# Hymba-style decoder step on one core: the up projection's seven-product scheme over all sixteen K tiles, operands and weight sums in place, residual summed in memory

## The chip, the cores and the metric

The kernel runs on one core of a Trainium2 chip. The time is device microseconds from one execution of the program, the median of three runs. The profile is of one further execution. Engines: TensorE (PE; its weight loads PEld), VectorE (DVE), ScalarE (ACT), GpSimd (POOL) and SyncE (SP), which here only issues transfers.

## What is computed

One layer over 512 prompt tokens and 8 x 4 sample tokens, 2048 channels, all in float32. Cut to what bears on this change:

```python
x = x + g1 * (concatenate([a_out, o]) @ w_out)             # output projection, residual
h2 = rms_norm(x, norm_ffn_g) * (1 + sc2) + sh2             # sc2, sh2, g2 come from c @ w_ada
u, f_tail = causal_dwconv(f_prev, h2 @ w_up, ffn_conv_w, ffn_conv_b)   # 2048 -> 2 x 5632, width 3
gate, val = split(u, 2)
x = x + g2 * ((silu(gate) * val) @ w_down)                 # 5632 -> 2048
```

Before it stand the input projection, a convolution group, windowed attention and the copies of two caches into the outputs; the change leaves these as they are.

## The kernel before

Channels lie on the 128 partitions, tokens along the free axis: 544 columns in two halves of 272 (256 prompt, 16 sample). Each float32 product is three matmuls: a weight tile and an activation tile are each split into a rounded part and a remainder (`split`, L344: ScalarE casts, VectorE subtracts), and hi x hi, hi x lo, lo x hi are added in PSUM. A weight split covers four tiles (128x512) and has three buffers of each part; raw weights come in 512 KB loads on SP's queue into three buffers (`load_w`, L192).

The sequence of the second half: `rest()` is the output projection, with the residual in two SBUF tiles `x2` and the sum of squares kept on VectorE; then `rstd2`; then the last `w_ada` stage, whose sixteen loads go through four buffers `raw_g`; then the sixteen channel tiles are normalised and modulated (`modulate2`). Tiles 8 to 15 are split as they are (`h2hi`, `h2lo`). Tiles 0 to 7 become seven operands of four tiles each (`sthi`, `stlo`): a two by two block scheme (gate and value outputs by two halves of K against two halves of K by two column halves) that needs seven block products in place of eight.

Each of the 44 pairs `f` (one gate and one value channel tile, `up_mm`) does the seven products over eight K tiles, 84 matmuls of 272 columns, with weight sums in separate buffers, and `direct` products over the other eight, 96 matmuls, into the same PSUM banks. The first pair takes its plain part from an array of its own (`w_up0`) before the seven products. Results are placed into `us` tiles; `up_conv` is the convolution (ScalarE the first tap, VectorE two more), then silu, product and split. After the first pair of each chunk of four comes the down product of the chunk before it (`down`): sixteen output tiles of 24 matmuls, each added with its gate into `x2` by VectorE (`gated_add`); the last one stores `x2` as the output `o_y` through ScalarE's queue.

The order on each engine is set when the program is built: a scheduler goes by program order and by which instruction is ready in its own estimate; on the chip each engine then takes its list in order. `shift_cache` puts one 1022 KB cache copy, memory to memory, behind a weight load on SP's queue.

## Time and profile before

| | before |
|---|---|
| median of three runs | 2668.88 us (2662.72 to 2673.99) |
| profiled execution, its own time | 2669.57 us |
| its span, first to last instruction | 2667.8 us |
| TensorE busy | 2603.1 us, 98%, 21073 matmuls |
| VectorE busy | 1655.6 us, 62% |
| ScalarE busy | 1082.9 us, 41% |
| GpSimd busy | 163.4 us, 6% |
| moved by DMA | 517.5 MB, mean 194 GB/s |

Matmuls are pipelined, so the mean time of one (about 290 ns) is longer than the distance between two; a stretch divided by its count of matmuls gives what one costs. The share of an engine is an average over stages with different limits.

### The profile page before, as it was taken

Reading aid. Unit: us, or ns where it says so; the run is one execution under the profiler, and the core shown is the slowest. Engines: PE = TensorE matmul, PEld = TensorE weight load, DVE = VectorE, ACT = ScalarE, POOL = GpSimd, SP = SyncE. Lnnn points to the kernel's source line nnn. Section 1 sums busy time; section 2 is a strip of 40 time slices with the busy share of each in tenths; the row PEclk is TensorE's granted clock in tenths of the full one; section 3 lists DMA queues with packets and bytes.
Section 4 is the critical chain, followed back from the end, with each engine's and each line's share of the span. In section 5 each row is a group of like instructions: output and inputs, shape, how many; then the busy total and the mean of one; then the engine's idle time right before and its main releaser. Section 6 shows DMA issues by size and latency. Waiting matters only on the chain.

```text
span 2667.8 us, 51885 instructions
## 1 busy us (share of the span) xinstructions
PE 2603.1 (98%) x21073; PEld 2380.3 (89%) x21073; DVE 1655.6 (62%) x3312; ACT 1082.9 (41%) x2069; POOL 163.4 (6%) x448
## 2 busy tenths in 40 slices
PE   6999999999999999789999999999999999999999
PEld 5878676778767799589999999999999999999999
DVE  5678754635665343676676766665757676666665
ACT  4355554445447332443343424242424242434332
POOL 0000000000000000010010101010101010100000
PEclk8999999999999999899999999999999999999999
DMA  9885567676764542445554555455455555554554
GB/s 352 278 277 160 187 199 261 227 257 226 244 224 158 179 153 88 142 163 192 182 191 167 192 182 191 167 192 182 173 185 192 182 173 186 190 183 169 192 186 140
DMA packets 119135, 517.50 MB, mean 194 GB/s; under 512 B 15728, under 2 KB 25584, under 8 KB 116080
## 3 DMA queue, kind: packets, MB, share of 16 engines
q1 hardware_dynamic: 103744, 494.98, 54.3%
q10 hardware_dynamic: 15152, 19.22, 2.1%
q8 instruction: 165, 2.70, 0.4%
q14 instruction: 74, 0.61, 0.1%
HBM read 503.18 MB, written 144.92 MB: 243 GB/s over the span
## 4 chain that ended last, share of the span: by engine, by line
PE 95%; DVE 2%; DMA 2%; ACT 1%; issue 0%; DVEq 0%; ACTq 0%
PE acc L207 47%; PE b L887 36%; PE x L272 4%; PE x L706 2%; PE x L657 2%; PE m L515 1%; PE m L445 1%; DMA raw_s<-w_ada 1%; PE m L480 1%; PE acc L324 1%; PE m L477 1%; PE m L498 1%; DMA raw_g<-w_ada 0%; DVE slo L346 0%; DVE qkr L320 0%
## 5 line engine op out<-in xcount | busy, mean ns | idle before, releaser
L345 ACT CAST whi<-raw_w 128x512 fp32r<-128x512 f32 x752 | 466.0, 620 | 888.9 <-PE acc L207 684.5
L346 DVE TENSOR_TENSOR wlo<-raw_w,whi 128x512 fp32r<-128x512 f32 x752 | 517.2, 688 | 347.5 <-ACT whi L345 336.6
L207 PE MATMUL acc<-hhi,whi 128*128 128x272 f32 x1792 | 393.1, 298 | 2.7 <-ACT hhi L345 2.3
L887 PE MATMUL b<-dhi,whi 128*128 128x272 f32 x1376 | 394.7, 289 | 0.0
L887 PE MATMUL b<-dlo,whi 128*128 128x272 f32 x1376 | 392.8, 288 | 0.0
L887 PE MATMUL b<-dhi,wlo 128*128 128x272 f32 x1376 | 384.3, 289 | 0.0
L207 PE MATMUL acc<-hhi,wlo 128*128 128x272 f32 x1792 | 382.6, 292 | 0.0
L207 PE MATMUL acc<-hlo,whi 128*128 128x272 f32 x1792 | 380.4, 292 | 0.0
L887 PE MATMUL b<-shi,whi 128*128 128x272 f32 x1232 | 358.5, 291 | 17.0 <-ACT whi L345 8.4
L887 PE MATMUL b<-slo,whi 128*128 128x272 f32 x1232 | 356.2, 289 | 1.5 <-DVE slo L346 1.5
L887 PE MATMUL b<-shi,wlo 128*128 128x272 f32 x1232 | 357.4, 290 | 0.0
L207 PEld LDWEIGHTS acc<-hhi,whi 128*128 128x128 f32 x1792 | 282.5, 189 | 53.2 <-issue 39.6
L207 PEld LDWEIGHTS acc<-hhi,wlo 128*128 128x128 f32 x1792 | 283.0, 190 | 22.4 <-issue 20.9
L207 PEld LDWEIGHTS acc<-hlo,whi 128*128 128x128 f32 x1792 | 283.2, 189 | 21.0 <-issue 18.5
L337 DVE SCALAR_TENSOR_TENSOR half<-acc,modT,half 128x512 f32<-128x512 f32 x200 | 150.1, 750 | 244.8 <-PE acc L207 244.7
L207 PE MATMUL acc<-alo,whi 128*128 128x272 f32 x1408 | 291.6, 288 | 0.0
L207 PE MATMUL acc<-ahi,whi 128*128 128x272 f32 x1408 | 290.6, 288 | 0.8 <-DVE tg L340 0.5
L207 PE MATMUL acc<-ahi,wlo 128*128 128x272 f32 x1408 | 290.9, 288 | 0.0
L887 PEld LDWEIGHTS b<-dlo,whi 128*128 128x128 f32 x1376 | 259.4, 189 | 0.0
L887 PEld LDWEIGHTS b<-dhi,whi 128*128 128x128 f32 x1376 | 259.3, 188 | 0.0
L887 PEld LDWEIGHTS b<-dhi,wlo 128*128 128x128 f32 x1376 | 253.5, 188 | 0.1
L887 PEld LDWEIGHTS b<-shi,whi 128*128 128x128 f32 x1232 | 232.8, 189 | 19.1 <-ACT whi L345 8.7
(207 smaller groups left out, 3694.5 us busy)
## 6 DMA issues: line engine op xcount, KB each, us to landing
raw_s<-w_ada SPq DMA_DIRECT2D x176, 512.0 KB, 4.8
raw_w<-w_up SPq DMA_DIRECT2D x176, 512.0 KB, 3.7
o_k_s<-cache_k SPq DMA_DIRECT2D x64, 1022.0 KB, 6.9
o_v_s<-cache_v SPq DMA_DIRECT2D x64, 1022.0 KB, 6.6
raw_w<-w_down SPq DMA_DIRECT2D x88, 512.0 KB, 3.7
raw_w<-w_in SPq DMA_DIRECT2D x80, 512.0 KB, 4.3
raw_s<-kT_c SPq DMA_DIRECT2D x64, 448.0 KB, 4.3
raw_s<-v_c SPq DMA_DIRECT2D x56, 512.0 KB, 4.5
```

What stands on the lines that cost most here:

```text
L207: nc.tensor.matmul(out[:, c, 0:HALF], lhsT=w, rhs=x[:, c, :], start=start and i == 0, stop=stop and i == 2)
L272: nc.tensor.matmul(ps[32 * j:32 * j + 9, 0:w], lhsT=silc[:, kt, :], rhs=t[:, c:c + w], start=kt == 0, stop=kt == KT - 1)
L324: nc.tensor.matmul(ps[:, c, 0:HALF], lhsT=w, rhs=src[:, c, :], start=start, stop=stop)
L337: nc.vector.scalar_tensor_tensor(pv(dst), pv(ps), modT[:, gate, 0:1], pv(dst), op0=ALU.mult, op1=ALU.add)
L345: nc.scalar.copy(hi, src)
L346: return nc.vector.tensor_tensor(lo, src, hi.bitcast(F32), op=ALU.subtract).ins
L445: nc.tensor.matmul(s_ps[:, 0:HALF], lhsT=blk, rhs=sq[:, c, :], start=True, stop=True)
L477: nc.tensor.matmul(s_ps, lhsT=lq, rhs=kr[rows[par], :, 0:HP], start=True, stop=True)
L480: nc.tensor.matmul(s_ps[:, 0:n0], lhsT=lq, rhs=kr[rows[par], 0, 0:n0], start=True, stop=True)
L657: nc.tensor.matmul(s_ps[32 * g:32 * g + 32, 0:hk], lhsT=qb[:, 2 * g + o, n, :], rhs=ks[g], start=o == 0 and n == 0, stop=o == 1 and n == 1 ...
L706: nc.tensor.matmul(o_ps[32 * g:32 * g + 32, :], lhsT=pT[0:w, c0:c0 + 32], rhs=rhs[g], start=kt == 0, stop=kt == 7)
L887: nc.tensor.matmul(out[:, 0:HALF], lhsT=w, rhs=x, start=start and i == 0, stop=stop and i == 2, skip_group_check=True)
```

## The change

- The seven-product scheme now covers all sixteen K tiles: seven operands of eight tiles (`B1`, `B2`, `T1` to `T3`; `T4` takes the place of the second half of `B1`). A pair is 7 x 8 x 3 = 168 matmuls. The first two pairs are plain products over all tiles and both halves (`direct`), 192 matmuls each.
- Normalisation, modulation and the block sums of the operands are done in place in `x2`, two or four tiles at a time, during the plain pairs: `plain` before each quarter of the first, `while_sums` before each quarter of the second. The convolution and product of these two pairs (`gated_act`) come after the pools they need are open, the first before the third pair, the second after it.
- Weight sums are done in place in the raw tiles, 1024 wide, with one extra tile `s1`; raw weights have two buffers more (`load_u`), and the loads' order is a11, a21, a22, a12.
- `x` is written to `o_y` during the output projection (`finished`); a down product's result is scaled by ScalarE into a tile `ym` (three buffers) and added into `o_y` in memory by an accumulating transfer issued by GpSimd.
- Twelve of the last `w_ada` stage's loads are issued during the output projection, the last square goes to the sum over partitions by itself, and pools are opened in another order.

```diff
-RAW_G = 4
-Q = 4
-XN = 3
+RAW_G = 12
+Q = 8
+YM = 3
...
+    mid.close()
+    o1 = ctx.enter_context(ExitStack())
     op = pool("op", bufs=4, to=o1, side="right")
+    o2 = ctx.enter_context(ExitStack())
+    og = pool("og", bufs=RAW_G, to=o2, side="right")
+    psf = pool("psf", bufs=4, space=PSUM)
     x2.append(half_tile())
...
+    def finished(m):
+        nc.scalar.dma_start(A["o_y"][m], x2[m // 8][:, m % 8])
...
+            finished(m)
+            if m < KT - 1:
+                sumsq(ssum2, x2[m // 8][:, m % 8], op, False)
+    last_ada = len(FIRST) + 7
+    raw_g = []
+    loads = ada_loads(last_ada, lambda: og.tile([P, 1024], F32, name="raw_g"))
+    for i, _ in enumerate(rest()):
+        if i >= 10 and len(raw_g) < RAW_G:
+            raw_g.append(next(loads))
+    ada = ada_stage(psf, op, last_ada, chain(raw_g, loads), main_ps())
+    for _ in range(6):
+        next(ada)
+    sq = wtile(op)
+    nc.scalar.activation(sq, x2[1][:, 7], AF.Square)
     ps = main_ps()
-    ones_sum(ps, ones, ssum2)
+    ones_sum(ps, ones, ssum2, True, False)
+    ones_sum(ps, ones, sq, False, True)
+    rstd2 = op.tile([P, 2, HALF], F32, name="ssum", bufs=1)
     rstd_from(ps, D, op, rstd2)
+    run(ada)
+    o2.close()
     hs.close()
+    fs = ctx.enter_context(ExitStack())
     hf = pool("hf", to=fs)
...
+    B1, B2 = operand("b1", 2), operand("b2", 2)
+    T1, T2, T3 = operand("t1"), operand("t2"), operand("t3")
+    B11, B21, B22, T4 = ([t[:, i] for t in b] for b, i in ((B1, 0), (B2, 0), (B2, 1), (B1, 1)))
+    def normalized(h, j, n):
+        x = x2[h][:, j:j + n]
+        v = x.rearrange("p k c n -> p k (c n)")
+        r = rstd2.rearrange("p (o c) n -> p o (c n)", o=1).broadcast_to([P, n, 2 * HALF])
+        nc.vector.tensor_tensor(v, v, r, op=ALU.mult)
+        k = 8 * h + j
+        for c in range(2):
+            xs = x[:, :, c, HP:HALF].rearrange("p k (b t) -> p k b t", t=DT)
+            for base, alu in ((SC2, ALU.mult), (SH2, ALU.add)):
+                m = modT[:, base + k:base + k + n, 1 + 4 * c:5 + 4 * c].rearrange("p k (b o) -> p k b o", o=1)
+                nc.vector.tensor_tensor(xs, xs, m.broadcast_to([P, n, DB // 2, DT]), op=alu)
+        for i in range(n):
+            nc.scalar.activation(pv(x[:, i]), pv(x[:, i]), AF.Identity, bias=modT[:, SH2 + k + i, 0:1],
+                                 scale=modT[:, SC2 + k + i, 0:1])
+    def blocks(h, j, n):
+        src = x2[h][:, j:j + n].rearrange("p k c n -> p c k n")
+        hi, lo = (b[:, :, j:j + n] for b in (B1, B2)[h])
+        split(hi, lo, src)
+    def combine(j, n):
+        b11, b12, b21, b22 = (x2[h][:, j:j + n, c] for h in range(2) for c in range(2))
+        nc.vector.tensor_tensor(b11, b12, b11, op=ALU.subtract)
+        yield
+        split(T1[0][:, j:j + n], T1[1][:, j:j + n], b11)
+        yield
+        nc.vector.tensor_tensor(b12, b22, b12, op=ALU.subtract)
+        yield
+        split(T3[0][:, j:j + n], T3[1][:, j:j + n], b12)
+        yield
+        nc.vector.tensor_tensor(b22, b22, b11, op=ALU.subtract)
+        yield
+        split(T2[0][:, j:j + n], T2[1][:, j:j + n], b22)
+        yield
+        nc.vector.tensor_tensor(b21, b21, b22, op=ALU.subtract)
+        yield
...
+    def direct(f, outs, before):
+        for h in range(2):
+            raws = [load_w(A["w_up"][t, h]) for t in (f, FT + f)]
+            shift_cache(raws[1][1])
+            for u in range(2):
+                before(h, u)
+                ws = [split_w(raw[:, u]) for raw, _ in raws]
+                for a in range(4):
+                    k = 4 * u + a
+                    for out, (hi, lo) in zip(outs, ws):
+                        for c in range(2):
+                            mm1(out[c], hi[:, a], lo[:, a], *(b[:, c, k] for b in (B1, B2)[h]),
+                                h == 0 and k == 0, h == 1 and k == 7)
+    for j in range(0, 4, 2):
+        normalized(0, j, 2)
+    def plain(h, u):
+        for j in (0, 2):
+            blocks(h, 4 * u + j, 2)
+            if (h, u) != (1, 1):
+                normalized(h + u, 4 * (1 - u) + j, 2)
+    first = [[bank(), bank()] for _ in range(2)]
+    direct(0, first, plain)
+    o1.close()
+    fe = pool("fe", to=fs)
...
+    def load_u(src):
+        nraw[0] += 1
+        if nraw[0] % 5 in (2, 4):
+            raw = fe.tile([P, 1024], F32, name="raw_x", bufs=2)
+            ins = nc.sync.dma_start(raw, src).ins
+            return raw.rearrange("p (u a m) -> p u a m", u=2, m=P), ins
+        return load_w(src)
...
+    st_in = state_tile(0)
+    us0 = placed(first, st_in, 0)
+    second = [main_ps(), main_ps()]
+    sums = chain(combine(0, 4), combine(4, 4))
+    def while_sums(h, u):
+        for _ in range(4):
+            next(sums, None)
+    direct(1, [[t[:, c] for c in range(2)] for t in second], while_sums)
+    run(sums)
+    for j in (0, 4):
+        split(T4[0][:, j:j + 4], T4[1][:, j:j + 4], x2[1][:, j:j + 4, 0])
+    hx.close()
+    fp = pool("fp", to=fs, side="right")
+    def product(out, w, b, start, stop):
+        for u in range(2):
+            hi, lo = split_w(w[:, u])
+            for a in range(4):
+                k = 4 * u + a
+                mm1(out, hi[:, a], lo[:, a], b[0][:, k], b[1][:, k], start and k == 0, stop and k == 7)
...
+    def up_mm(f, usg, usv):
+        a11, _ = load_u(A["w_up"][f, 0])
+        a21, _ = load_u(A["w_up"][FT + f, 0])
+        a22, ins = load_u(A["w_up"][FT + f, 1])
         shift_cache(ins)
-        a11, a12, a21, a22 = g0[:, 0], g0[:, 1], v0[:, 0], v0[:, 1]
-        s1, s2, s4 = (fp.tile([P, 4, P], F32, name="sum", bufs=3) for _ in range(3))
+        a12, ins = load_u(A["w_up"][f, 1])
+        shift_cache(ins)
+        s1 = fe.tile([P, 2, 4, P], F32, name="sum", bufs=1)
         b1 = bank()
-        product(b1, a11, 0, True, True)
+        product(b1, a11, B11, True, True)
         nc.vector.tensor_tensor(s1, a21, a22, op=ALU.add)
-        nc.vector.tensor_tensor(s2, s1, a11, op=ALU.subtract)
+        nc.vector.tensor_tensor(a21, a11, a21, op=ALU.subtract)
+        nc.vector.tensor_tensor(a11, s1, a11, op=ALU.subtract)
         b2 = bank()
-        product(b2, s2, 4, True, True)
-        p1 = part_tile("p1")
+        product(b2, a11, T2, True, True)
+        p1 = part_tile("p1", 2)
         nc.scalar.copy(p1, b1[:, 0:HALF])
         u2 = part_tile("u2")
         plus(u2, b2[:, 0:HALF], p1)
-        product(b1, a12, 1, False, early)
-        nc.vector.tensor_tensor(a21, a11, a21, op=ALU.subtract)
-        product(b2, a21, 5, False, True)
+        product(b1, a12, B21, False, True)
+        nc.vector.tensor_tensor(a12, a12, a11, op=ALU.subtract)
+        place(usg, 0, copied, b1)
+        product(b2, a21, T3, False, True)
         u3 = part_tile("u3")
         plus(u3, b2[:, 0:HALF], p1)
-        b4 = None
-        if not early:
-            b4 = bank()
-            g1, _ = load_w(A["w_up"][f, 1])
-            direct((b1, b4), g1, (False, True), (True, False))
-        place(usg, 0, copied, b1)
         b3 = bank()
-        product(b3, s1, 3, True, True)
+        product(b3, s1, T1, True, True)
         plus(u2, b3[:, 0:HALF], u2)
-        nc.vector.tensor_tensor(s4, a12, s2, op=ALU.subtract)
-        if early:
-            b4 = bank()
-        product(b4, s4, 2, early, True)
+        place(usv, 1, plus, b3, u3)
+        b4 = bank()
+        product(b4, a12, B22, True, True)
         place(usg, 1, plus, b4, u2)
         b5 = bank()
-        product(b5, a22, 6, True, early)
-        if not early:
-            v1, ins = load_w(A["w_up"][FT + f, 1])
-            shift_cache(ins)
-            direct((b5, b3), v1, (False, False), (True, True))
-        place(usv, 1, plus, b3, u3)
+        product(b5, a22, T4, True, True)
         place(usv, 0, plus, b5, u3)
...
+    def gated_act(f, usg, usv, tails, j):
         gt = up_conv(f, usg, tails, 2 * j)
         vl = up_conv(FT + f, usv, tails, 2 * j + 1)
         nc.scalar.activation(gt, gt, AF.Silu)
...
-    def down(c, last):
+    def up_pair(f, st_in, tails, j):
+        usg, usv = us_tile(st_in, 2 * j), us_tile(st_in, 2 * j + 1)
+        up_mm(f, usg, usv)
+        gated_act(f, usg, usv, tails, j)
+    def down(c):
         for mp in range(8):
-            raw, ins = load_w(A["w_down"][c, mp])
+            raw, ins = load_u(A["w_down"][c, mp])
             if mp % 2:
                 shift_cache(ins)
             for j in range(2):
...
                 for k in range(CHUNK):
                     ahi, alo = acts[CHUNK * c + k]
                     mm3(ps, hi[:, k, :], lo[:, k, :], ahi, alo, k == 0, k == CHUNK - 1)
-                xm = x2[m // 8][:, m % 8]
-                gated_add(xm, ps, G2 + m, fp)
-                if last:
-                    nc.scalar.dma_start(A["o_y"][m], xm)
+                ym = fp.tile([P, 2, HALF], F32, name="ym", bufs=YM)
+                nc.scalar.activation(pv(ym), pv(ps), AF.Copy, scale=modT[:, G2 + m, 0:1])
+                nc.vector.tensor_tensor(sv4(ym), sv4(ps), per_batch(modT[:, G2 + m, 1:9]), op=ALU.mult)
+                nc.gpsimd.dma_start(A["o_y"][m], ym, accum_op=ALU.add)
 
     for c in range(NCHUNK):
-        st_in = fp.tile([P, 2 * CHUNK, DB, 2], F32, name="st_in", bufs=2)
-        nc.scalar.dma_start(st_in, A["state_f"][c])
-        tails = fp.tile([P, 2 * CHUNK, 9, 2], F32, name="tails", bufs=2)
-        for j in range(CHUNK):
+        if c:
+            st_in = state_tile(c)
+        tails = fe.tile([P, 2 * CHUNK, 9, 2], F32, name="tails", bufs=2)
+        if c == 0:
+            gated_act(0, *us0, tails, 0)
+        for j in range(2 if c == 0 else 0, CHUNK):
             up_pair(CHUNK * c + j, st_in, tails, j)
+            if c == 0 and j == 2:
+                gated_act(1, *placed([[t[:, i] for i in range(2)] for t in second], st_in, 1), tails, 1)
             if c and j == 0:
-                down(c - 1, False)
+                down(c - 1)
         nc.scalar.dma_start(A["o_fc"][c], tails)
-    down(NCHUNK - 1, True)
+    down(NCHUNK - 1)
```

## Rows read from the trace of the kernel before

**Rows 1.** The page, part 1: busy us, share of the span, instructions.
```profile
PE 2603.1 (98%) x21073; PEld 2380.3 (89%) x21073; DVE 1655.6 (62%) x3312; ACT 1082.9 (41%) x2069; POOL 163.4 (6%) x448
```

**Rows 2.** The page, part 4: the chain that ended last, by engine and line.
```profile
PE 95%; DVE 2%; DMA 2%; ACT 1%; issue 0%; DVEq 0%; ACTq 0%
PE acc L207 47%; PE b L887 36%; PE x L272 4%; PE x L706 2%; PE x L657 2%; PE m L515 1%; PE m L445 1%; DMA raw_s<-w_ada 1%; PE m L480 1%; PE acc L324 1%; PE m L477 1%; PE m L498 1%; DMA raw_g<-w_ada 0%; DVE slo L346 0%; DVE qkr L320 0%
```

**Rows 3.** Stretches: length, busy PE, PEld, DVE, ACT, POOL (instructions), PE clock, DMA share, GB/s.
```profile
1088.50:1245.30 156.80, 132.42 (x1029) 120.69 (x1029) 118.81 (x246) 78.40 (x131) 15.56 (x40) 0.90 0.50 174
1245.30:2613.40 1368.10, 1367.41 (x10859) 1366.69 (x10858) 894.63 (x1849) 500.64 (x862) 109.89 (x310) 1.00 0.53 183
```

**Rows 4.** The page, part 5: costliest groups (count; busy us, mean ns; idle before).
```profile
L345 ACT CAST whi<-raw_w 128x512 fp32r<-128x512 f32 x752 | 466.0, 620 | 888.9 <-PE acc L207 684.5
L346 DVE TENSOR_TENSOR wlo<-raw_w,whi 128x512 fp32r<-128x512 f32 x752 | 517.2, 688 | 347.5 <-ACT whi L345 336.6
...
L887 PE MATMUL b<-dhi,whi 128*128 128x272 f32 x1376 | 394.7, 289 | 0.0
...
L887 PE MATMUL b<-shi,whi 128*128 128x272 f32 x1232 | 358.5, 291 | 17.0 <-ACT whi L345 8.4
```

**Rows 5.** Stretches: four consecutive up pairs.
```profile
1433.60:1524.10 90.50, 90.50 (x721) 90.50 (x720) 61.34 (x115) 39.64 (x71) 10.29 (x28) 1.00 0.54 190
```

**Rows 6.** Timeline of VectorE in an up pair (start us, us, instruction).
```profile
1474.37 0.69 DVE L929 TENSOR_TENSOR sum<-sum,raw_w 128x512 f32<-128x512 f32 x1
1474.97 0.69 DVE L346 TENSOR_TENSOR wlo<-raw_w,whi 128x512 fp32r<-128x512 f32 x1
```

**Rows 7.** Timeline after the output projection.
```profile
1090.85 0.72 DVE L320 TENSOR_TENSOR ssum<-ssum,w 128x544 f32<-128x544 f32 x1 [0.72 <-ACT w L319]
...
1095.86 0.72 DVE L306 SCALAR_TENSOR_TENSOR rstd<-w 128x544 f32<-128x544 f32 x1
1096.62 2.00 DVE L327 TENSOR_TENSOR xn<-half,rstd 128x544 f32<-128x544 f32 x3
...
1097.38 2.22 ACT L328 ACTIVATE xn<-xn,modT 128x512 f32<-128x512 f32 x3 [3.07 <-DVE xn L327]
...
1098.53 0.39 DVE L329 TENSOR_TENSOR xn<-xn,modT 128x32 f32<-128x32 f32 x3
```

**Rows 8.** VectorE's groups by form, 1433.6 to 1572.7 us.
```profile
L978 DVE SCALAR_TENSOR_TENSOR ca<-us,fw,ca 128x560 f32<-128x560 f32 x16 | 12.8, 799 | 1.8 <-ACT ca L976 1.7
...
L346 DVE TENSOR_TENSOR alo<-a,ahi 128x544 fp32r<-128x544 f32 x4 | 2.9, 717 | 0.0
...
L1000 DVE TENSOR_TENSOR a<-ca 128x512 f32<-128x512 f32 x4 | 2.7, 685 | 0.0
```

**Rows 9.** Stretches between the output projection and the up pairs.
```profile
1120.00:1130.00 10.00, 3.67 (x20) 2.61 (x18) 9.97 (x25) 7.34 (x12) 0.00 (x0) 0.80 0.00 0
...
1100.00:1140.00 40.00, 24.08 (x178) 16.96 (x174) 33.22 (x81) 23.94 (x37) 0.00 (x0) 0.76 0.30 100
```

**Rows 10.** The chain in order of time: start us, us, what.
```profile
1157.13 12.88 PE b L887 x99
```

**Rows 11.** Stretches: inside the output projection.
```profile
1040.00:1060.00 20.00, 20.00 (x162) 20.00 (x161) 8.01 (x15) 5.66 (x9) 0.00 (x0) 1.00 0.32 101
```

**Rows 12.** Issue of the stores of y: ns least, median, most.
```profile
L1027 ACTq DMA_DIRECT2D o_y<-half x16: 338/338/343, 2622.5 to 2664.8; - x16
```

**Rows 13.** Timeline of the end, VectorE.
```profile
2663.70 0.75 DVE L337 SCALAR_TENSOR_TENSOR half<-acc,modT,half 128x512 f32<-128x512 f32 x1 [1.94 <-PE acc L207]
```

**Rows 14.** DMA issues: count, KB each, median us to landing.
```profile
raw_w<-w_up SPq DMA_DIRECT2D x176, 512.0 KB, 3.7
o_k_s<-cache_k SPq DMA_DIRECT2D x64, 1022.0 KB, 6.9
...
o_y<-half ACTq DMA_DIRECT2D x16, 272.0 KB, 2.2
```

**Rows 15.** GpSimd's copies into the tails tile: ns least, median, most.
```profile
L973 POOL COPY tails<-us x88: 184/719/1391, 1155.3 to 2614.4; 128x2 f32<-128x2 f32 x88
```

More of the change, by code (lines that the diff above doesn't have):

```diff
@@ L175, in build @@
     g_ffn = params[:, 96 + KT:96 + 2 * KT]
[L176 removed]
+    cw = f32(qkp, [P, CT, W_CONV + 3], "cw")
     nc.scalar.dma_start(cw, A["conv_a"])
@@ L256, in interleave, with ada_loads, ada_stage @@
                 next(side, None)
-    def ada_stage(psp, tmp, s, get=None):
-        get = get or raw_tile
+    def ada_loads(s, get):
+        n = ADA_STAGES[s][2]
+        for i in range(KT * n // 4):
+            t = get()
+            nc.sync.dma_start(t, A[f"w_ada{s}"][i])
+            yield t
+    def ada_stage(psp, tmp, s, loaded=None, banks=None):
         t_a, t_b, n = ADA_STAGES[s]
@@ L263, in ada_stage @@
         per = 1024 // (groups * w)
-        ps = psp.tile([P, 512], F32, name="x", bufs=XB)
+        ps = banks[:, 0] if banks is not None else psp.tile([P, 512], F32, name="x", bufs=XB)
+        loaded = loaded or ada_loads(s, raw_tile)
         for i in range(KT // per):
-            t = get()
-            nc.sync.dma_start(t, A[f"w_ada{s}"][i])
+            t = next(loaded)
             for k in range(per):
@@ L279, in ada_stage @@
             copy(st[32 * j:32 * j + 9, 0:w], ps[32 * j:32 * j + 9, 0:w])
-        pt = psp.tile([P, 512], F32, name="m")
+        pt = banks[:, 1] if banks is not None else psp.tile([P, 512], F32, name="m")
         ns, nj = w // P, groups // 2
@@ L888, in mm1, with us_tile @@
                              skip_group_check=True)
[L890 to L902 removed]
+    def direct(f, outs, before):
[22 more added lines that the diff above has]
+    fe = pool("fe", to=fs)
+    fw = f32(fe, [P, UT, 4], "fw")
+    nc.scalar.dma_start(fw, A["ffn_conv"])
+    nraw = [0]
+    def load_u(src):
[5 more added lines that the diff above has]
+        return load_w(src)
+    def us_tile(st_in, slot):
+        us = fe.tile([P, UW], F32, name="us", bufs=2)
+        seg = us[:, USEG:].rearrange("p (b w) -> p b w", w=2 + DT)
+        nc.gpsimd.memset(us[:, 0:2], 0.0)
+        nc.gpsimd.tensor_copy(seg[:, :, 0:2], st_in[:, slot])
+        return us
     def place(us, c, op, ps, t=None):
@@ L915, in copied, with state_tile, placed @@
         nc.scalar.copy(out, ps)
-    def part_tile(name):
-        return fp.tile([P, HALF], F32, name=name, bufs=1)
-    def up_mm(f, usg, usv, early):
-        g0, _ = load_w(A["w_up"][f, 0])
-        v0, ins = load_w(A["w_up"][FT + f, 0])
+    def state_tile(c):
+        st_in = fe.tile([P, 2 * CHUNK, DB, 2], F32, name="st_in", bufs=2)
+        nc.scalar.dma_start(st_in, A["state_f"][c])
+        return st_in
+    def placed(outs, st_in, j):
+        uss = [us_tile(st_in, 2 * j + i) for i in range(2)]
+        for us, out in zip(uss, outs):
+            for c in range(2):
+                place(us, c, copied, out[c])
+        return uss
```

85 lines of the change are left out of this document (13 added, 72 removed).

## The prediction

> **What bounds the kernel now.** I read the shares of the engines first: TensorE is busy 98% of the span, VectorE 62% [rows 1]. Then the chain of waits: 95% of what ends last is TensorE, 47% its lines of projections and down products, 36% the line of the up products [rows 2]. Last the stretches: from the first down product (1245.3 us) to the end of the last up pair (2613.4 us) TensorE is busy 1367.4 of 1368.1 us at full clock, so there a matmul costs 1368.1 / 10859 = 0.126 us and nothing else counts. Before it, from the end of the output projection (1088.5) to 1245.3, it is busy 132 of 156.8 us at a mean clock of 0.90 [rows 3]. That is the one stretch where waits cost: 900 up matmuls at 0.126 are 113 us, so 43 us go to other things. The profiled execution took 2669.57 us, 0.7 over the median of the runs; I sum on it and take 0.7 off.
>
> **The change part by part.**
>
> *Fewer matmuls.* Of the old up projection the plain half is 3 x 1376 matmuls, the seven-product half 3 x 1232 [rows 4]; with 96 of the first pair that another line issues, 7920, or 180 a pair. New: two plain pairs of 192 (16 K tiles, two outputs, two column blocks, three terms), and 42 pairs of 7 x 8 x 3 = 168, in all 7440. The tile shape stays 128x272. In the TensorE-bound stretch stand 39 pairs: 39 x 12 x 0.126 = **59 us less**. The other 12 fall into the transition.
>
> *VectorE in a steady pair.* Four consecutive pairs take 90.5 us, VectorE 61.3 in them [rows 5], 15.3 a pair. A 512-wide operation starts 0.60 us after the one before it [rows 6], and three 544-wide ones take 2.00 us together, 0.64 apart [rows 7]; from the two, 1.1 ns an element, so one 1024 wide takes 1.16 us (at most 1.21, two narrow ones) and one 1088 wide 1.23. A pair now has 14 weight splits for 11 (+1.8) and four 1024-wide weight sums for four 512-wide (+2.2): 19.3 us in a pair of 168 x 0.126 = 21.2 us. VectorE is still hidden, but at 91%, not 68%. What is late next is the pair's second product: its weight difference (1.16) must wait until the first product's splits have read the tile it overwrites, and its own cast (0.62) and low part (0.69) follow [rows 4], while VectorE also has the convolution of the pair before, about 4.1 us (four taps 0.7 apart, product, split) [rows 8]. With three split buffers the second product's operand can be started about 1.5 us before the pair begins and is wanted at 3.0 us. Followed by hand it is between 0 and 0.75 us late, at the 29 of 39 pairs that don't follow a down product. Lower end 0 (nothing idles now). Upper end: VectorE no busier than 33.2 of 40 us, as it was where it set the pace [rows 9]; then a pair takes 19.3 / 0.83 = 23.3 us, 2.1 more, 61 us in all. I take 0.4 x 29 = **12 us**, near the lower end, since the work fits, and where enough stood ready VectorE was 9.97 of 10 us busy [rows 9].
>
> *Transition.* Now: last output product at 1088.5, square, sum and three Newton steps to 1096.6, then sixteen modulations, differences and splits on VectorE, until the up products run without a break from 1157 [rows 10]. New: the last square goes straight to TensorE (one 0.72 addition less), so the scale is there at 1095.9 [rows 7]; the w_ada products run under it, since twelve of sixteen loads are requested during the output projection, whose DMA share is 0.32 [rows 11]. These loads and sixteen stores of x pass SP's and ScalarE's queues there; they are hidden by that free share, and uncovered their issue alone would cost 28 x 0.34 = 9.5 us [rows 12]. First operands: two-tile product 1.23, sample columns 0.4, ScalarE 2 x 0.74, a cast of twice the width of one that takes 0.62 [rows 4], so 1.24 at most, and its low part 1.23: TensorE starts near 1101.5. VectorE then has, for plain pair one, 16 wide operations of 1.23, 32 small ones of 0.10 and 8 splits of 0.60: 27.7 us against 24.2 of TensorE; for plain pair two, 16 wide ones and 8 splits, 24.5 against 24.2; then two pairs of 19.3, with the two delayed convolutions, 8.2. Sum 99 us from 1095.9, then one more pair of 21.2 to the first down product: 1216 with VectorE never idle, 1236 at the 83% of [rows 9]. TensorE alone would allow 1101.5 + 888 x 0.126 = 1213. I take the middle of the VectorE figures, 1226, against 1245.3: **19 us less** (9 to 32).
>
> *Residual in memory.* A down product's evacuation leaves VectorE (0.75 us [rows 13]) for ScalarE (0.81, as its 512-wide scaling row [rows 7]) and a small VectorE multiply; ScalarE then has 0.62 + 0.81 of each 3.02 us, hidden under TensorE. GpSimd issues 176 accumulating transfers of 272 KB; behind each stand the zeroing and state copies of the next pair's tiles, wanted only 9 us into that pair. Three buffers allow 3 x 3.02 = 9.1 us from one use to the next, less 0.8 for ScalarE: 8.2 us for issue and landing. No row shows an accumulate. From below, the plain 272 KB store of y lands in 2.2 us; from above, a 1022 KB copy, memory to memory, in 6.9 [rows 14]. Both fit; I take 4 to 5, nearer the store by size, and nothing on the path. At the very end it shows: the last product ends at 2663.7 [rows 13], and 0.75 + 0.3 + store become 0.81 + issue + accumulate: **+2 us** (0 to +5).
>
> *Loads.* Five raw buffers for three; a pair holds four, the last until its seventh product's split, about 3.2 us before the pair ends. The next pair's fourth tile is requested then and wanted 6 us into it, against the 3.7 us to landing of such a load [rows 14]: nothing, or, if a cache copy is ahead of it, part of the 12 us above.
>
> Sum: 2669.6 - 59 - 19 + 12 + 2 = 2605.6, less 0.7: about **2605 us**.
>
> **The rivals.**
>
> *VectorE becomes the bound* (for it: 91% and longer chains; against: a long unbroken supply of splits). At 83% in both places: 2669.6 - 59 - 9 + 61 + 2 = 2665 us, no change.
>
> *The accumulates are too slow: slower.* If one takes longer than 8.2 us from issue to landing, ScalarE waits for the buffer, with the casts of the next weights behind it, and TensorE waits for both; each of 176 products takes a third of the excess longer. It decides from 8.2 + 3 x (64 / 176) = 9.3 us; at 12 us it costs 176 x 1.27 = 223 us: 2829 us. Against it: both transfers of [rows 14] lie below. For it: GpSimd's own rows, a two-element copy taking 0.18 to 1.39 us, median 0.72 [rows 15]. The Trainium skill (SBUF — State Buffer, section "Who interferes with whom") says that a VectorE instruction with two SBUF inputs holds the shared interface, and a GpSimd instruction that reads SBUF is blocked for its whole length, while one that only writes is not; the spread of that row agrees, and whether issuing an accumulate reads is shown by no run here. By the rule a blocked issue would use 1.2 of the 8.2 us and move the deciding landing to 8.1.
>
> *TensorE alone sets the pace in both places:* no wait in the pairs and 1213 for the first down product: 2669.6 - 59 - 32 + 2 = 2581 us. For it: 0.7 us idle in 1368 now; against: VectorE's 99 us in the transition.
>
> **How the numbers follow.** Forecast 0.68 (its own range 2588 to 2632), VectorE the bound 0.12, slow accumulates 0.06, TensorE alone 0.14. The range 2580 to 2650 leaves out the accumulates, half of the VectorE case and a tail below. Within 0.5% (13 us, about what a measurement tells from no change) lies the upper half of the VectorE case, 0.05; slower are the accumulates and a little of that case, 0.07; faster 0.88.
>
> **What would show it right or wrong.** Right: 7440 matmuls on the line of the up products; a pair of 21.2 to 21.6 us, four plus a down product in about 134 us for 139; VectorE 85 to 92% busy within pairs; the first down product between 1213 and 1236; o_y landing in 3 to 7 us with no wait of ScalarE on it. Wrong: TensorE idle at the start of second products with a low-part release from VectorE for over 2 us a pair; a low granted clock inside the pairs; ScalarE waiting for a y buffer; the first down product after 1245.

## The result: 2.6% slower

Median 2740.41 us (2729.78 to 2743.93, four runs) against 2668.89 (2662.72 to 2673.99): ratio 1.0262 (95% interval 1.0227 to 1.0298). The forecast was 2605 us, with a range of 2580 to 2650. The profiled execution took 2729.78 us, 10.6 under its median; the sums below are made on it, against 2669.57 us before.

### The profile page after: what moved, and what is told of

Same layout as the page of the kernel before. It is cut to its first block, busy times and chain, and to the rows that moved or that the text cites. A ratio compares the mean times of both kernels' runs of the same rounds, so it can differ in the third digit from the quotient of the medians.

```text
span 2728.0 us, 51730 instructions
## 1 busy us (share of the span) xinstructions
PE 2583.4 (95%) x20597; PEld 2342.4 (86%) x20597; DVE 1677.4 (61%) x3029; ACT 1258.3 (46%) x2371; POOL 332.4 (12%) x624
## 4 chain that ended last, share of the span: by engine, by line
PE 67%; DVE 12%; DMA 10%; issue 6%; ACT 3%; POOL 1%; SPq 0%; DVEq 0%; ACTq 0%; POOLq 0%
PE acc L209 38%; PE b L933 18%; DVE wlo L354 4%; DMA raw_w<-w_up 4%; PE x L280 3%; DMA o_y<-ym 3%; DMA raw_x<-w_up 2%; ACT whi L353 2%; DVE ca L1078 2%; PE x L714 2%; PE x L665 2%; PE m L523 1%; DVE us L992 1%; ACT ca L1076 1%; DMA raw_g<-w_ada 1%
## 5 line engine op out<-in xcount | busy, mean ns | idle before, releaser
L354 DVE TENSOR_TENSOR wlo<-raw_x,whi 128x512 fp32r<-128x512 f32 x270 | 183.2, 687 | 121.9 <-ACT whi L353 119.6
L209 PEld LDWEIGHTS acc<-ahi,whi 128*128 128x128 f32 x1408 | 224.4, 192 | 33.7 <-DVE ym L1119 32.5
L209 PEld LDWEIGHTS acc<-alo,whi 128*128 128x128 f32 x1408 | 225.3, 192 | 0.2 <-DVE alo L354 0.2
L209 PEld LDWEIGHTS acc<-ahi,wlo 128*128 128x128 f32 x1408 | 224.8, 191 | 0.0
L933 PE MATMUL b<-b2hi,whi 128*128 128x272 f32 x704 | 205.8, 292 | 9.9 <-ACT whi L353 9.9
L933 PE MATMUL b<-b2hi,wlo 128*128 128x272 f32 x704 | 205.8, 293 | 8.7 <-DVE wlo L354 8.6
L933 PE MATMUL b<-b1hi,wlo 128*128 128x272 f32 x704 | 205.5, 295 | 2.2 <-DVE wlo L354 2.2
L933 PE MATMUL b<-b1hi,whi 128*128 128x272 f32 x704 | 204.0, 292 | 1.3 <-ACT whi L353 1.0
L933 PE MATMUL b<-b1lo,whi 128*128 128x272 f32 x704 | 204.6, 292 | 0.1
L933 PE MATMUL b<-b2lo,whi 128*128 128x272 f32 x704 | 203.3, 289 | 0.0
```

The costliest lines, as they stand in the source:

```text
L209: nc.tensor.matmul(out[:, c, 0:HALF], lhsT=w, rhs=x[:, c, :], start=start and i == 0, stop=stop and i == 2)
L354: return nc.vector.tensor_tensor(lo, src, hi.bitcast(F32), op=ALU.subtract).ins
L933: nc.tensor.matmul(out[:, 0:HALF], lhsT=w, rhs=x, start=start and i == 0, stop=stop and i == 2, skip_group_check=True)
```

## The profile after

The page, part 1 and part 4 (for [rows 1, 2]): TensorE has 476 records fewer and a smaller share; a third of the chain now belongs to others.

```profile
PE 2583.4 (95%) x20597; PEld 2342.4 (86%) x20597; DVE 1677.4 (61%) x3029; ACT 1258.3 (46%) x2371; POOL 332.4 (12%) x624
...
PE 67%; DVE 12%; DMA 10%; issue 6%; ACT 3%; POOL 1%; SPq 0%; DVEq 0%; ACTq 0%; POOLq 0%
```

The two stretches of [rows 3], now from the end of the output projection (1095.9 us for 1088.3) to the first down product, and from there to the end of the last up pair, with the same columns:

```profile
1095.90:1249.10 153.20, 130.52 (x1030) 121.65 (x1029) 121.61 (x199) 83.45 (x138) 17.86 (x39) 0.92 0.48 168
1249.10:2668.00 1418.90, 1348.84 (x10394) 1325.99 (x10393) 926.20 (x1646) 661.77 (x1139) 263.10 (x472) 0.99 0.70 206
```

Two up pairs of the steady part, for [rows 5]; an idle-free pair would take 168 x 0.126 = 21.2 us. VectorE is 85% and 89% busy in these stretches, TensorE 92%:

```profile
1618.00:1642.00 24.00, 22.16 (x168) 21.40 (x168) 20.46 (x35) 12.03 (x23) 3.54 (x10) 1.00 0.49 176
1642.00:1666.00 24.00, 21.96 (x170) 21.50 (x170) 21.30 (x37) 12.42 (x22) 3.63 (x9) 1.00 0.54 182
```

From the single matmuls I add up, between the first down and the last up product, each distance from one start to the next that is over 0.2 us, less 0.126; "idle" below is this sum, given to the product that starts. The rest of the time is still 0.125 to 0.126 us a matmul.

| | before | after |
|---|---|---|
| output projection ends | 1088.3 | 1095.9 |
| from there to the first down product | 156.8 | 153.2 |
| up matmuls in the steady stretch | 7020 | 6552 |
| idle of the up products | 1.6 | 68.7 |
| idle of the down products | 0.0 | 42.4 |
| last up product to the end of the span | 54.3 | 60.0 |

The span's 60.2 us are 7.6 - 3.6 - 59 + 67 + 42 + 6. What the matmuls saved is there; two kinds of idle time, 109 us, took it back.

The idle of the up products varies between runs by itself. Three runs below that leave the up pairs as they are (e2, e4, e8) show 77 to 83 us, and the 68.7 here come from the fastest of four executions. A difference of up to some 15 us in it shows nothing.

**Where the down products idle.** The chain of waits in one down product (start us, us, what):

```profile
1566.24 6.95 DMA raw_w<-w_up
...
1573.28 0.06 DVE sum L1045
1573.34 0.09 issue
1573.42 0.02 DVEq L1046
1573.44 0.97 issue
1574.42 0.20 DVE ym L1119
1574.61 0.04 issue
1574.66 14.75 PE acc L209 x96
```

VectorE's timeline beside it (start us, us, instruction, idle before it and what ended that):

```profile
1568.52 0.69 DVE L354 TENSOR_TENSOR wlo<-raw_x,whi 128x512 fp32r<-128x512 f32 x1 [2.21 <-ACT whi L353]
1573.28 1.23 DVE L1045 TENSOR_TENSOR sum<-raw_w 128x1024 f32<-128x1024 f32 x1 [4.07 <-DMA raw_w<-w_up]
1574.42 0.18 DVE L1119 TENSOR_TENSOR ym<-acc,modT 128x32 f32<-128x32 f32 x1
```

VectorE stands idle for 4.07 us before the first weight sum of the *next* up pair, whose load takes 6.95 us to land. At the ten down products that an up pair follows, the load that this sum waits for takes 4.3 to 7.9 us; in the kernel before, the same one took 3.4 to 4.3. In VectorE's list that sum is ahead of several of the small y multiplies of the down product that is running; TensorE waits for the bank that such a multiply empties. The waits in this stretch (engine, for whom; us in total, times, longest) name another culprit:

```profile
DVE ym L1119 <- ACT ym L1118: 44.8, 31, 2.7
...
ACT ym L1118 <- DMA o_y<-ym: 40.9, 28, 2.7
DVE sum L1045 <- DMA raw_w<-w_up: 35.8, 20, 5.0
```

ScalarE waits 28 times for a y buffer, that is for an accumulate to land (page, part 6, for [rows 14]; single ones 3.9 to 10.3 us):

```profile
raw_w<-w_up SPq DMA_DIRECT2D x109, 512.0 KB, 4.3
o_y<-ym POOLq DMA_DIRECT2D x176, 272.0 KB, 5.2
```

**Where the up products idle.** 53 of the 69 us lie in the second product: 27 before its first matmul (29 gaps), the rest within it, where TensorE's list already has some of the third's. 13 us lie in the sixth. The chain up to a second product:

```profile
1601.25 4.21 DMA raw_w<-w_up
...
1605.59 0.13 DVE sum L1045
...
1607.68 1.22 DVE raw_x L1046
...
1612.87 0.03 DVE ca L1078
1612.90 0.69 issue
1613.59 0.69 DVE wlo L354
1614.28 0.71 DVE ca L1078
1614.99 0.41 DVE us L992 x2
1615.41 1.13 DVE raw_w L1047
1616.54 0.74 DVE ca L1078
1617.28 0.02 issue
1617.30 0.70 DVE wlo L354
1618.00 0.04 issue
1618.05 2.03 PE b L933 x14
```

This chain holds both suspects: a load, and VectorE's list after it, in which the convolution's taps (`ca`) stand around the difference (L1047) that the second product needs.

## The experiments

Theories: **V**, VectorE has too much to do in an up pair; **L**, loads come late, since the raw tiles are held by the differences in place; **A** (with **D**, a shortage of DMA time in a down product), the accumulating transfers cost by themselves; **H** (formed later), they only delay loads, and the waiting sum does the rest. All ratios are to the kernel before on the same chip. Idle times are in us.

| run | median us | ratio, 95% interval | idle down | idle up |
|---|---|---|---|---|
| new kernel | 2740.4 | 1.0262 (1.0227 to 1.0298) | 42.4 | 68.7 |
| e1_copies_up | 2749.9 | 1.0306 (1.0287 to 1.0324) | 50.4 | 82.3 |
| e2_plain_store | 2704.3 | 1.0129 (1.0096 to 1.0162) | 11.7 | 77.6 |
| e3_product_order | 2725.3 | 1.0207 (1.0182 to 1.0232) | 32.4 | 81.9 |
| e4_ada_early | 2732.7 | 1.0240 (1.0209 to 1.0270) | 43.0 | 82.9 |
| e6_before_accum | 2691.0 | 1.0095 (1.0079 to 1.0111) | 21.2 | 0.8 |
| e7_no_taps | 2670.2 | 1.0018 (1.0001 to 1.0034) | 31.8 | 23.3 |
| e8_six_ym | 2718.2 | 1.0190 (1.0160 to 1.0221) | 15.8 | 77.0 |
| e9_more_raw | 2728.8 | 1.0232 (1.0215 to 1.0249) | 48.8 | 63.3 |
| e10_gpsimd_one | 2751.7 | 1.0305 (1.0282 to 1.0327) | 39.8 | 90.1 |
| e11_gpsimd_two | 2762.0 | 1.0347 (1.0328 to 1.0366) | 53.7 | 94.9 |
| e12_joined | 2809.3 | 1.0520 (1.0505 to 1.0536) | 23.5 | 157.1 |
| r12_joined_vector | 2729.2 | 1.0233 (1.0203 to 1.0263) | 30.0 | 82.5 |
| r13_no_taps_six_ym | 2661.4 | 0.9984 (0.9968 to 0.9999) | 18.1 | 26.7 |
| r14_twelve_tiles | 2716.1 | 1.0180 (1.0159 to 1.0201) | 27.2 | 31.7 |
| r15_before_accum_six | 2694.5 | 1.0095 (1.0071 to 1.0119) | 22.0 | 1.3 |
| r16_sums_behind | 2756.9 | 1.0330 (1.0310 to 1.0350) | 10.6 | 124.4 |
| r17_before_accum_behind | 2721.7 | 1.0206 (1.0182 to 1.0231) | 4.7 | 39.1 |
| r18_sums_two_back | 2702.8 | 1.0134 (1.0112 to 1.0157) | 10.5 | 74.2 |

### The down products

**Copies out of the down products.**
```diff
-            if mp % 2: shift_cache(ins)          # in down()
-        shift_cache(ins)                         # after a12's load
+        shift_cache(ins, 2)
```


> The four cache copies of each down product are moved to the up pairs (three a pair for two); nothing else. Theory D: a down product is short of DMA time. Counted by the packets of the changed kernel's trace, one engine of the sixteen needs 8 loads x 8 x 0.20 + 4 copies x 2.7 + 16 accumulates x 8 x 0.22 = 52 us in a stage of 48 us; without the copies 41 us. Then TensorE's idle time in the down products falls from 42 to under 10 us, the accumulates land in under 6 us, and the time falls by 30 to 40 us against the changed kernel, to about 2705. Rival R (an accumulate's own latency with three buffers): idle stays above 30 us, time about 2735. The up pairs, with one copy more each, are unchanged or up to 10 us slower in both.

The idle of the down products is 50 us, not under 10: four copies fewer in one did not free it, and D as priced there fell. The up pairs, with four copies more, idle 82 us, no more than e4 with its copies where they were.

**A plain store in place of the accumulate.**
```diff
-                nc.gpsimd.dma_start(A["o_y"][m], ym, accum_op=ALU.add)
+                nc.gpsimd.dma_start(A["o_y"][m], ym)
```


> The down products are stored into y without accumulating, so y holds the last chunk's product alone; all else as in the changed kernel. Theory D: a plain 2176-byte packet took 0.09 us against 0.22, so the DMA time in a down product falls to 12.9 + 10.8 + 11.8 = 36 us of 48; idle in the down products under 5 us for 42, time about 2700. If instead it is GpSimd's issue (0.86 us each) or the buffer count, the idle time stays above 25 us. The up pairs keep their 69 us of idle time in every case.

The down idle is 12 us for 42, and the median 36 us lower: it is the accumulating, not the number of transfers. (An issue also took GpSimd 0.54 us for 0.86, which no run takes apart from it.) TensorE's wait for y multiplies fell from 26.8 to 7.3 us, and the load of the next pair's first sum took 3.9 to 5.3 us.

**That part alone, in the kernel before.**
```diff
-                gated_add(xm, ps, G2 + m, fp)
+                ym = fp.tile([P, 2, HALF], F32, name="ym", bufs=3)
+                ...
+                nc.gpsimd.dma_start(A["o_y"][m], ym, accum_op=ALU.add)
```


> The kernel before with one part of the change alone: the residual stored while the output projection runs, x freed after the modulations, and each down product scaled into one of three y buffers and added in memory by an accumulating transfer. Theory A (the accumulates cost DMA time of their own: 16 in a down product at 1.78 us of all sixteen engines, 28 us, with its loads and copies 52 us against 48 us of TensorE): the down products idle 30 to 45 us in all, median 2698 to 2712 us, though the up pairs here have slack. Rival C (they cost only in the new kernel, whose loads come late because the raw tiles are held): down idle under 10 us, median 2665 to 2680 us.

This is 25 us slower than the kernel before, a third of the whole loss: the down products idle 21 us, though the up pairs here have slack.

**Six y buffers, in either kernel.**
```diff
-    T1, T2, T3 = operand("t1"), operand("t2"), operand("t3")   # new kernel only: makes room
+    T1, T2 = operand("t1"), operand("t2"); T3 = T1
-YM = 3
+YM = 6
```


> The new kernel with six y buffers for three; to make room the third and the first difference of activations share one tile (wrong y, same instructions). If what the down products wait for is the spread of single accumulates (3.9 to 10.3 us to land against 8.2 us that three buffers allow), their idle falls from 42 us to under 15, median 2705 to 2718 us. Theory A (the transfers of a down product need more of the DMA engines than TensorE's 48 us): the queue only grows longer, idle stays over 30, median 2728 to 2742 us. Idle of the up products 65 to 80 by both.

> The kernel before with the residual in memory, as in the sixth run, with six y buffers for three. If the accumulates cost by the spread of their landing alone: idle of the down products falls from 21 to under 6 us, median 2668 to 2676 us. If the DMA engines are short in a down product (52 us of work in 48): idle stays over 15 us, median 2685 us or more.

In the new kernel the idle fell to 16 us, as if buffers were short; in the kernel before it stayed at 22, as for A. Neither theory fits both. The chain of the second of these runs (r15) showed why: no ScalarE wait for a buffer is left, yet

```profile
1422.01 6.00 DMA raw_w<-w_up
...
1428.03 0.04 DVE sum L936
...
1428.64 0.19 DVE ym L1034
1428.83 0.04 issue
1428.88 7.82 PE acc L209 x48
```

A load of 6.00 us, a weight sum, a y multiply, TensorE: the new kernel's chain. From this came H.

**The sums moved in VectorE's list.**
```diff
+                last_ym[0] = nc.vector.tensor_tensor(sv4(ym), ...).ins   # down(); r18: only m == 13
...
+        with tc.issue_after(last_ym[0]):
             nc.vector.tensor_tensor(s1, a21, a22, op=ALU.add)             # up_mm, and the differences behind it
```


> The sixth run (the kernel before with the residual in memory, three y buffers) with one thing moved: in VectorE's list the weight sums of the pair that follows a down product stand behind the last y multiply, not ahead of the last four. Theory H (an accumulate costs nothing by itself; the transfers make the next pair's loads land late, and the sum that waits for such a load holds the y multiplies behind it and by them the banks of TensorE): idle of the down products falls from 21 to under 6 us, median 2668 to 2678 us. Theory A (the transfers themselves): idle stays over 15 us, 2685 us or more.

> The new kernel with the same move: the three weight sums of the pair after a down product behind the last y multiply. Theory H: the wait of the banks for y multiplies (27 us) goes, that for y buffers (41 us of ScalarE's waits, a part of it on the path) stays: idle of the down products from 42 to 15 to 25 us, of the up products up by 0 to 8 us, median 2712 to 2728 us. Theory A: no change, 2735 us or more.

> The new kernel with the three weight sums of the pair after a down product behind the fourteenth of its sixteen y multiplies (the planner's list has the first of them ahead of the last six, the run before this one behind the last). If the sum's place is what the down products pay for, and there is a place that suits both: idle of the down products from 42 to 10 to 20 us as in the run before, and the up products stay at 65 to 75 us: 2705 to 2722 us. If the wait only moves from one to the other: the two together stay over 100 us, 2733 us or more.

Behind the last y multiply the down idle went, 21 to 5 and 42 to 11 us, as H says. The medians rose all the same, to 2721.7 and 2756.9 us, where A had put them: now the second product behind a down product waits for its sum (in r17 by 2.5 us, ten times), and the up idle is 39 and 124 us. Two multiplies earlier both are served: down idle 10.5, up idle 74, **2702.8 us, 38 less than the new kernel**, by the place of three sums in a list. ScalarE's wait for y buffers did not fall with it, it doubled:

```profile
ACT ym L1125 <- DMA o_y<-ym: 85.0, 58, 3.7
...
PE acc L209 <- DVE ym L1126: 6.2, 10, 1.9
```

So the wait that bears the accumulate's name costs next to nothing here; moving the sums took away 32 us of idle time that it did not name.

### The up pairs

**Products reordered**, those on raw tiles first, so that each sum has a product more of time.
```diff
-        a11·B11, (s1-a11)·T2, a12·B21, (a11-a21)·T3, s1·T1, (a12-s2)·B22, a22·T4
+        a11·B11, a22·T4, a12·B21, (s1-a11)·T2, (a11-a21)·T3, s1·T1, (a12-s2)·B22
```


> The seven products of a pair in another order: the plain tiles first (a11 B11, a22 T4, a12 B21), then T2, T3, T1, B22, with the loads in the order in which the tiles are used and given back. VectorE's work is the same. Theory O: the pairs lose time because the second product needs a chain of three sums whose inputs land late, while VectorE still has the convolution before. Then the idle time in the up pairs falls from 69 to under 20 us and the time to about 2690. Rival V (VectorE has too much work in a pair, 91% by the count): idle stays above 50 us, time 2725 to 2740. The down products keep their 42 us in both.

The up idle is 82 us, no less: the gaps moved to the later products, as V says. The median is 15 us lower, with intervals that touch.

**VectorE's taps left out.**
```diff
-        for j in (1, 2):
-            nc.vector.scalar_tensor_tensor(acc, us[:, j:j + UN], fw[:, m, j:j + 1], acc, op0=ALU.mult, op1=ALU.add)
```


> The new kernel without the convolution's two VectorE taps (y is not the reference's): four VectorE instructions of 0.7 us, 2.9 us, less in each pair, all loads and buffers as they are. Theory V (the up pairs idle because VectorE has too much to do in them): idle of the up products falls from 69 us to under 35, median 2695 to 2712 us. Rival L (they idle because the raw tiles are held until the differences in place have been read, so loads come late): idle stays over 55, median 2728 to 2742 us.

2.9 us less VectorE in a pair, 45 us less up idle, 70 us off the median (some of it in the down products and the transition). V holds. What it leaves open is whether the taps cost by their time or by their place around the difference: no run moves them in the list.

**More raw buffers.**
```diff
-        if nraw[0] % 5 in (2, 4):        # raw_x bufs=2, sum bufs=1
+        if nraw[0] % 7 in (0, 2, 4, 6):  # raw_x bufs=4, sum bufs=2
```


> The new kernel with seven raw weight buffers for five and two sum tiles for one, room made as in the run beside it (first and third difference of activations share a tile; wrong y, same instructions). Rival L (late loads): idle of the up products falls from 69 us to under 30, median 2690 to 2705 us. Theory V (VectorE's work): idle stays over 50, median 2722 to 2742 us.

The up idle is 63 us, not under 30: L fell as a cause of its own.

**Sums on GpSimd**, which is 12% busy: one, and two of the four.
```diff
-        nc.vector.tensor_tensor(a12, a12, a11, op=ALU.subtract)
+        nc.gpsimd.tensor_tensor(a12, a12, a11, op=ALU.subtract)
```


> The new kernel with one of the four weight sums of a pair (a12 -= a11, 1024 wide, wanted by the sixth product) on GpSimd instead of VectorE. Theory V with a free GpSimd: VectorE has 1.2 us less in each pair, 40% of what the taps were, so idle of the up products falls from 69 to about 50 us and the median to about 2712 us. Rival S (GpSimd gets at SBUF only between VectorE's instructions): the difference takes over 5 us on GpSimd and comes late, idle over 75 us, median 2740 us or more. The Trainium skill (SBUF - State Buffer, Who interferes with whom) speaks for S.

> As the run beside it, with the difference for the fourth product (a21 = a11 - a21) on GpSimd too. Theory V with a free GpSimd: 2.3 us less of VectorE in each pair, 80% of the taps, idle of the up products about 32 us, median about 2685 us. Rival S: the fourth product waits for GpSimd, idle over 100 us, median 2765 us or more.

Neither gains: the median is 2752 us with one, its interval overlapping the new kernel's, and 2762 with two, clear of it. The difference that takes VectorE 1.22 us takes GpSimd 2.40, and while it runs VectorE's own instructions grow: groups of the run with one (busy us, mean ns, idle before), GpSimd's first. The two low parts took 687 and 724 ns in the new kernel; the second takes 2098 with two sums moved.

```profile
L1055 POOL TENSOR_TENSOR raw_w<-raw_w 128x1024 f32<-128x1024 f32 x15 | 36.0, 2400 | 38.9 <-DVE wlo L354 38.9
...
L354 DVE TENSOR_TENSOR wlo<-raw_w,whi 128x512 fp32r<-128x512 f32 x346 | 259.0, 761 | 156.8 <-ACT whi L353 151.5
...
L354 DVE TENSOR_TENSOR alo<-a,ahi 128x544 fp32r<-128x544 f32 x36 | 42.4, 1178 | 5.0 <-ACT ahi L353 3.0
```

The Trainium skill (SBUF — State Buffer, "Who interferes with whom") says that a VectorE instruction with two SBUF inputs and a GpSimd instruction that reads SBUF exclude one another. The trace agrees on VectorE's side, 761 ns for 687; what GpSimd's difference would take undisturbed is shown by no run.

**A dose between the kernels**: before, with the residual in memory and seven products over 12 of 16 K tiles.
```diff
-Q = 4                                    # K tiles a block; 180 matmuls a pair
+Q = 6                                    # 174; four K tiles plain, two in each raw tile; w_up's tiles reordered
```


> A dose between the two kernels, and the whole computation: from the kernel before, the residual in memory, and the seven products over twelve of the sixteen K tiles, six a block; 174 matmuls a pair (180 before, 168 in the new kernel), five y buffers, six raw buffers. VectorE: 1.0 us more in low parts and 1.2 in sums than the 15.3 us of a pair before, 17.5 of 21.9, 80%. Theory V: at 80% the up products idle under 15 us; 39 x 6 x 0.126 = 29 us less, +4 for VectorE in the transition, +12 for the accumulates: about 2654 us, under both kernels. Rival (what idles is the chain of sums and late loads itself, at any share of VectorE): idle over 40 us, 2690 us or more.

This run has five y buffers and six raw ones. Its idle is between both expectations: 32 us in the up products, 0.8 a pair, against 0.04 before and 1.8 in the new kernel. From one down product to the next (four pairs) VectorE is busy 76% in this run and 82% in the new kernel, where it was 68% before [rows 5]; the run's line first:

```profile
1458.30:1548.50 90.20, 87.73 (x689) 86.46 (x689) 68.72 (x133) 46.19 (x91) 9.77 (x29) 1.00 0.57 197
...
1593.30:1683.80 90.50, 86.09 (x666) 84.17 (x666) 74.37 (x127) 46.27 (x82) 12.30 (x28) 1.00 0.57 193
```

The idle grows with the share, and the saving of 29 us is gone at 76%. The run without taps fits in: 75%, 0.6 us a pair. The down idle here (27 us) comes from sums ahead of y multiplies again, and the transition is 16 us longer than before (more operands to make), so the median says less than the idle.

### The transition, and the gains together

**The last w_ada stage inside the output projection**, one load behind each weight load, not twelve at once.
```diff
-RAW_G = 12
+RAW_G = 4
+            with tc.issue_after(pinned[0]):      # the w_out unit before it
+                nc.sync.dma_start(t, A[f"w_ada{last_ada}"][i])
```


> The last w_ada stage is done inside the output projection as in no kernel so far: one load pinned behind each w_out load, four buffers, the products two steps later. Theory P: the changed kernel's output projection ends 7.6 us late because twelve w_ada loads were queued at once ahead of a w_out load, and the normalisation starts late because VectorE's list has the stage's copies first, which wait for the last four loads. Then the output projection with the w_ada products ends near 1097 us, the first normalisation starts near 1105 (1110 in the changed kernel), and the first down product near 1240 (1249): time 2725 to 2732. Rival: the wait only moves to the first split (same VectorE work), first down product 1247 to 1250, time 2738.

The first down product starts at 1244.5 us for 1249.1, half of what was expected, and the median is 8 us lower, with intervals that overlap. That is no gain shown: e2 and e8, which leave the requests of these loads as they are, start it at 1244.6 and 1244.8. What the run does show is that the requests held the output projection up: from 950 to 1088 us TensorE is now busy all the time, with most of the w_ada products among it; the new kernel's line first:

```profile
950.00:1088.00 138.00, 130.65 (x1007) 129.77 (x1007) 51.55 (x101) 35.30 (x57) 0.00 (x0) 0.98 0.49 175
...
950.00:1088.00 138.00, 138.00 (x1125) 129.25 (x1125) 51.51 (x101) 35.78 (x57) 0.00 (x0) 0.99 0.58 190
```

**Joined**: that, the new product order and four y buffers, with and without two sums on GpSimd (both with one buffer fewer of `p1`, `st_in` and `tails`); and both causes lifted.

> What helped so far, joined, and the whole computation: the products in the order of the third run, the last w_ada stage inside the output projection, four y buffers, and two differences on GpSimd. By theory V with a free GpSimd: 2740 - 15 (order) - 8 (w_ada) - 55 (VectorE's work) - 10 (a fourth buffer) = about 2652 us, under the kernel before (2667). By rival S: over 2735 us.

> What helped, joined, with all sums back on VectorE: the products in the order of the third run, the last w_ada stage inside the output projection, four y buffers. If the three gains add: 2740 - 15 (order) - 8 (w_ada) - 10 (a third of what six buffers gave) = about 2707 us. By theory V the order and the buffers only move VectorE's work about: idle of the up products stays over 65 us, 2715 to 2730 us. Under 2667 us by neither.

> Both causes lifted at once in the new kernel: no VectorE taps and six y buffers (y and the convolution's outputs are not the reference's). If VectorE's work and the accumulates are two causes of their own: 2740 - 70 - 22 = about 2648 us, up products under 25 us idle and down products under 15. If the taps' gain was in part the accumulates' (they start from the same gaps): 2660 us or more.

The first is the slowest of all, the second gains 11 us where 33 were added up. Why is open: the gains of order and w_ada were not clear of the noise alone, and three buffers went. With both causes lifted the time is 2661 us, 79 under the new kernel where 92 were expected. No kernel that computes everything came under the one before (2667 us); the nearest with all sixteen K tiles in the scheme is r18_sums_two_back.

## Why the prediction was wrong

On the profiled executions the forecast was 2605.6 and the time 2729.8 us: 124 us, in three steps.

- *Fewer matmuls*, 59 us less: right. 468 of the 480 that go lie in the steady stretch and the price of one did not change.
- *VectorE in a steady pair*, +12: the mechanism was right, the size wrong, 67 us (miss 55). The work was sized well (18.8 us of VectorE a pair between down products, for 19.3), and the place was named, the start of the second product, but not its price: 29 gaps of 0.93 us for the 29 of 0.4, and then 26 us more within that product and 13 in the sixth, which the step gave no price. The failing sentence is "near the lower end, since the work fits". A share of work under 100% does not make a list in order free of waits: in the chain above VectorE first waits for a load and then works through a list, taps among it, that TensorE does not need yet. The upper end, 61 us from VectorE's 83% of [rows 9], was the better estimate, and the rival built on it (a pair of 23.3 us; 23.2 and 24.2 from one second product to the next in the stretches above) came out for this part. VectorE's share there is 82%; but 83% was borrowed from a stretch with other work, and no run shows it to be a limit, so that the figures agree so closely is partly luck.
- *Residual in memory*, "nothing on the path" and +2: it cost 42 + 6 (miss 46). The landing was forecast well, 4 to 5 us for 5.2, and the issue was 0.86 us (857 to 1013 ns), so hardly held up. But only one wait was looked at, the y buffer's. The step that failed is "nothing on the path": it priced the small VectorE multiply at nothing, and that multiply stands in VectorE's list behind the next pair's first sum. Before, that sum's load landed in 3.4 to 4.3 us and the place cost nothing; with accumulates on the same DMA engines it takes 4.3 to 7.9. The rival "accumulates too slow" named the y buffer and a landing of 9.3 us; the median landing stayed at 5.2, and r18 shows that the buffer's wait alone costs next to nothing.
- *Loads*, "nothing, or part of the 12": wrong by what it left out, that a load is late for its *place in a list*, not for its product.
- *Transition*, 19 less: 4 more (miss 23). 7.6 of it come before it, where the step called the moved loads "hidden by that free share": twelve w_ada loads were issued together ahead of the output projection's own. An average share of 0.32 [rows 11] says nothing of twelve requests in 15 us; the chain there:

```profile
949.23 0.45 SPq L265
...
949.72 14.21 DMA raw_g<-w_ada
...
965.61 0.46 PE acc L209
```

  The other 15 are the start. The last four w_ada loads went out only at 1096.9 to 1098.7 us, and VectorE's list has a copy of that stage (L287) first, so its first wide product starts at 1110.2, another 7 us late against the step's 1095.9. From there to the first down product it takes 138.9 us where the step had 130.1, the middle of its VectorE figures: 9 us. All seven wide products stand ahead of the first cast; the step had one there and TensorE at 1101.5, and its first up product came at 1123.2 (last line, from TensorE's timeline):

```profile
1098.71 9.11 DMA raw_g<-w_ada
...
1108.63 0.27 DVE ast L287
...
1110.17 8.48 DVE half L883 x7
...
1122.09 1.09 ACT b1hi L353
...
1123.23 1.05 PE L933 MATMUL b<-b1hi,whi 128*128 128x272 f32 x3 [0.38 <-ACT b1hi L353]
```

Shown by runs: V (e7 against e9 and e3), that the sum's place in the list makes the down idle (r16, r17, r18 against e6 and r15), and that the twelve requests held up the output projection (e4). Only read from the trace: the late start. Open: with both causes lifted 27 us of up idle are left, whose cause no run isolates; and why six buffers helped the new kernel while three suffice once the sum is moved. With six, the load that the sum waits for took 3.5 to 5.7 us, which would fit H, but no run separates the two waits there.

## What to carry to other kernels

A share of busy time under 100% is no cover for an engine that works through its list in order: ask of each instruction on it what stands *ahead* and what that waits for. When a change adds DMA work, look for instructions of the next stage, already in an engine's list, whose load used to land just in time; they hold up work that has nothing to do with the transfer. And where the profile names a wait, move something before you believe it: the named wait doubled in the run that won 38 us.

## What was not expected of the hardware

An accumulating packet of 2176 bytes keeps a DMA engine for 222 ns in the steady stretch, 9.8 bytes a ns; the plain stores of e2 moved packets of 4352 bytes in 174 ns, 25 bytes a ns. Sixteen accumulates of a down product are thus 28 us of all sixteen engines where plain ones are 11, and a neighbouring load shows it: the one that the first sum waits for takes 4.3 to 7.9 us with accumulates, 3.9 to 5.3 with plain stores, 3.4 to 4.3 with neither. A GpSimd difference of 128x1024 costs VectorE more than it takes off it: over 36 pairs the low parts above and their like on the other raw tiles grow by 53 us, 36 x 1.22 = 44 are saved.
